# Entering the first layer by quarters of its features, and summing the adaLN modulation on column strips of TensorE

## The chip, the cores and the metric

One Trainium2 chip, one core of it. The metric is the time of one execution of the whole kernel on the device, in microseconds (us), as the median of several runs. The profiled execution is one run more, taken by the hardware profiler.

TensorE is written PE here (PEld is its loading of weights), VectorE is DVE, ScalarE is ACT, GpSimd is POOL, and SP is the queue that issues most of the DMAs.

## The reference

The kernel computes two stacked blocks on 256 tokens of 1024 features, all in float32. The first block has two layers, and the change touches only the modulation and the norm at their entry, above all that of layer 0:

```python
def first_block(x, c, ada_w, ada_b, norm_g, ab_w_in, ...):
    cs = jax.nn.silu(c)                                  # c: 1 x 1024
    for layer in range(2):
        mod = cs @ ada_w[layer] + ada_b[layer]           # ada_w[layer]: 1024 x 3072
        shift, scale, gate = jnp.split(mod, 3, axis=-1)
        h = rms_norm(x, norm_g[layer]) * (1.0 + scale[:, None, :]) + shift[:, None, :]
        if layer % 2 == 0:
            y = even_mixer(h, ab_w_in[0], ab_w_out[0], ...)   # qa,ka,va | qb,kb,vb | g, two attentions
        else:
            y = odd_mixer(h, c_w_in[0], c_w_out[0], c_sink[0])
        x = x + gate[:, None, :] * y
    return rms_norm(x, final_g)
```

The second block (four mixers, then a gated FFN, twice) is not touched.

## The kernel before

**Matrix products.** Activations lie transposed, features on the 128 partitions in 8 chunks (`act`: a pair hi, lo of [128, 8, 256]). Each product of two float32 matrices is three matmuls on pairs of a rounded part and its remainder (`mm3`, L238 to L240). A weight unit of 128x1024 is fetched by SP into `wr`, rounded by ACT into `wh` (L220), and its remainder `wl` is a subtraction on DVE (L221). Products with features as output rows have 256 columns, those with tokens as output rows have 512.

**Order.** A scheduler writes down one order of instructions for each engine and for SP ahead of time, by priority; an engine then runs its list strictly in order, and an instruction whose input is late holds up all that stands behind it. Buffers rotate in pools: a new tile waits until the last reader of the buffer's earlier content is done. Small PSUM tiles (`mx`) come from a pool of 4 banks, products (`mm`) from one of 4.

**Modulation of layer 0, shift and scale** (`Mod.start`). It runs in two halves of 512 features. Rows of `ada_w` come in tiles of 128 rows x 512 columns (half 0: two row chunks in one DMA of 512 KB). Each row chunk k is to be multiplied by cs of its 128 rows and summed over k and over the partitions. The shift's chunks are summed over k on DVE (first chunk L434, then L436, an instruction of 128x512 each); of the scale's 8 chunks in half 0, the first 6 are summed on PE (L472; `csB` holds cs broadcast to 128 columns, so every output row is the full sum), the others on DVE. A matmul with ones (L481) then sums over the partitions and spreads the row to all partitions. norm_g of layer 0 is spread by a ones matmul too (L419, `gb`). G = norm_g*(1+scale) and the shift so stand as [128, 1024] tiles.

**First norm and first products** (`even_layer`). In each half, xn = x * rstd * G + shift (L597, L599) is built in pieces of 2 chunks by 2 token tiles, transposed on PE (L317), and split into hi (ACT, L321) and lo (DVE, L322). Then follow the products qa, ka (`proj_fm_part`) and va (`proj_tok_part`) over the 4 chunks of this half; the second half goes on adding to the same PSUM banks. After that the first attention begins with `sc` (L364, softmax on DVE L370 and ACT L373), `pt` (transposes of p, L382) and `pv` (L645), between products of qb, kb, vb and the gate.

**Later parts** (`Mod.part`): the gate of layer 0, and scale, shift and gate of layer 1, each in two halves. They are called one after the other from `later` while the attentions run: layer 0's gate and layer 1's scale and shift, 6 halves, in the even layer, layer 1's gate in the odd one. Each half fetches 8 tiles of 128x512 (`aw`, 3 buffers), sums them on DVE (L434, L436) into `macc`, adds the row of ada_b on POOL (L491), and ends with a ones matmul (L495).

**Layer 1's norm** (`AdaNorm`) uses layer 1's G and shift in row form, transposes at L317, and starts the odd layer's products.

Of the kernel before, what the change touches and what calls it, by code (L numbers as in the profile page):

```python
# [32 lines left out]
for _n, _l in ROWS:  # L33
# [4 lines left out]
        ("rwkv_r_k_2", 4), ("rwkv_v0_2", 2), ("hgrn_lb_logits_2", 4)]  # L38
# [318 lines left out]


# [45 lines left out]
class Mod:  # L404


    def __init__(self, n, l):
        self.n, self.l = n, l
        self.G = n.s2(f"G{l}", tag="mod")
        if l == 0:  # L410

            for half in range(2):
                s = slice(half * 512, half * 512 + 512)
                g = n.par("g1")[0:1, :]
                r = n.a["rows"]
                n.nc.scalar.dma_start(g, bass.AP(tensor=r.tensor, offset=r.offset + ROW_OFF["norm_g"] + half * 512,
                                                 ap=[[1, 1], [1, 512]]))
                ps = n.mx("gb")
                n.nc.tensor.matmul(ps, lhsT=n.ones[0:1, :], rhs=g, start=True, stop=True)  # L419
                n.nc.scalar.copy(self.G[:, s], ps)  # L420
        else:
            n.row_bc(self.G, "norm_g", l * D, D)
        self.shift, self.gate = n.s2(f"shift{l}", tag="mod"), n.s2(f"gate{l}", tag="mod")

    def src(self, part, half, k, m):
        w = self.n.a["ada_w"]
        ap = [[3 * D, 128], [128 * 3 * D, m], [1, 512]] if m > 1 else [[3 * D, 128], [1, 512]]
        return bass.AP(tensor=w.tensor, ap=ap,
                       offset=w.offset + self.l * D * 3 * D + k * 128 * 3 * D + part * D + half * 512)

    def add_k(self, acc, k, w, first):
        n, nc = self.n, self.n.nc
        if first:
            nc.vector.tensor_scalar(acc, w, n.cs[:, k:k + 1], None, op0=OP.mult)  # L434
        else:
            nc.vector.scalar_tensor_tensor(acc, w, n.cs[:, k:k + 1], acc, op0=OP.mult, op1=OP.add)  # L436
# [18 lines left out]
    def start(self, half, then=None):  # L455

        n, nc = self.n, self.n.nc
        bb = [self.row(part, half) for part in range(2)]
        ps = [n.mx("mod"), n.mx("mod")]
        acc = [n.s2("macc", tag="bias") for _ in range(2)]  # L460
        m, pe = (1, 0) if half else (2, 6)
        for k in range(0, 8, m):
            for part in (0, 1):
                if half:
                    rv = n.s2("aw").unsqueeze(1)
                else:
                    p, tag = (n.p_hi, "hi") if part else (n.p_lo, "lo")
                    rv = v2(p.tile([128, 1024], F32, name="aw", tag=tag))
                nc.sync.dma_start(rv if m > 1 else rv[:, 0, :], self.src(part, half, k, m))
                for j in range(k, k + m):  # L470
                    if part and j < pe:
                        nc.tensor.matmul(ps[1], lhsT=n.csB[:, j * 128:j * 128 + 128], rhs=rv[:, j - k, :],  # L472
                                         start=(j == 0), stop=False)
                    else:
                        self.add_k(acc[part], j, rv[:, j - k, :], j == pe * part)
                        if j == pe * part:
                            nc.vector.tensor_add(acc[part][0:1, :], acc[part][0:1, :], bb[part])
            if k == 2 and then:
                then()
        for part in (1, 0):  # L480
            nc.tensor.matmul(ps[part], lhsT=n.ones, rhs=acc[part], start=not (part and pe), stop=True)  # L481
            self.finish(part, half, ps[part])

    def part(self, part, half):
        n, nc = self.n, self.n.nc
        acc = n.s2("macc", tag="macc")
        for k in range(8):
            w = n.s2("aw", tag="aw")
            nc.sync.dma_start(w, self.src(part, half, k, 1))
            self.add_k(acc, k, w, k == 0)  # L490
        nc.gpsimd.tensor_add(acc[0:1, :], acc[0:1, :], self.row(part, half))  # L491

        def finish():
            ps = n.mx("mod")
            nc.tensor.matmul(ps, lhsT=n.ones, rhs=acc, start=True, stop=True)  # L495
            self.finish(part, half, ps)
        return finish

# [61 lines left out]
def even_layer(n, mod, later, follow):  # L560
# [24 lines left out]

    qk = [[n.mm() for _ in range(2)] for _ in range(2)]
    xn = [n.big("xn") for _ in range(2)]
    rs = []
    va = []
    for half in range(2):  # L590
        mod.start(half, None if half else n.load_x)
        if half == 0:
            rs = [n.norm_stat(t, xn[t]) for t in range(2)]
        for k in range(half * 4, half * 4 + 4, 2):
            s = slice(k * 128, k * 128 + 256)
            for t in range(2):
                nc.vector.scalar_tensor_tensor(xn[t][:, s], n.x[:, t, s], rs[t], mod.G[:, s], op0=OP.mult,  # L597
                                               op1=OP.mult)
# [1105 lines left out]
```

## Time and profile before

| what | value |
|---|---|
| median of 3 runs | 1337.56 us (1334.25 to 1338.48) |
| the profiled execution | 1340.15 us, of which the span from the first to the last instruction is 1338.4 us |
| PE busy | 1275.9 us, 95% of the span |
| DVE busy | 843.1 us, 63% |
| ACT busy | 647.6 us, 48% |
| POOL busy | 66.2 us, 5% |
| chain that ended last | PE 69%, DVE 9%, issue 5%, DMA 3% |
| TensorE's granted clock, mean | 0.987 |

A granted clock of 1 is 2.4 GHz and the lower level, 1.2 GHz, is 0.5; a mean between them says what share of the time was spent at each. The chain of work that ended last is followed back from the last instruction, at each step to what released it. In rows of the trace, `mm<-hh,wh` is an instruction that writes tile mm from hh and wh, `128*128` the rows and columns of the array that it uses, and `x4` says that four are shown as one row.

### The profile page before, as it was taken

The page shows a single profiled execution, that of the slowest core. Times are in us where ns is not written, and L with a number is a line of the kernel's source. Part 1 is how long each engine was busy: PE and PEld are TensorE (multiplying, and loading weights), DVE is VectorE, ACT ScalarE, POOL GpSimd, SP SyncE. Part 2 cuts the span into 40 slices and gives each one's busy share as a digit, 9 for nine tenths or more (in the row PEclk, how much of TensorE's full clock was granted, in tenths as well). Part 3 has the DMA queues.
Part 4 walks back from the last instruction along what each step waited for, and adds up shares of the span by engine and source line. Part 5 has one row for each costly group of instructions (what it writes and reads, how often), then busy time and mean ns, then how long its engine had stood idle before and what let it go on. Part 6 is the DMA issues. An engine that isn't in the chain of part 4 may idle for free.

```text
span 1338.4 us, 20297 instructions
## 1 busy us (share of the span) xinstructions
PE 1275.9 (95%) x7824; PEld 1101.6 (82%) x7824; DVE 843.1 (63%) x1438; ACT 647.6 (48%) x1093; POOL 66.2 (5%) x82
## 2 busy tenths in 40 slices
PE   6888889999899999999999999999999999999997
PEld 3777667888788888888899987988888887899986
DVE  6876897666658754666655544657753756655543
ACT  3364645665655345444544443556244444644432
POOL 0011110000111000000000000010000000000000
PEclk8898999999999999999999999999999999999999
DMA  8887765644552332365565554742331464655552
GB/s 303 302 268 269 245 215 181 200 141 131 173 167 87 105 96 90 103 215 180 174 186 183 181 188 142 229 146 91 94 112 64 149 199 155 201 179 186 186 186 86
DMA packets 104956, 227.19 MB, mean 170 GB/s; under 512 B 8206, under 2 KB 8350, under 8 KB 104860
## 3 DMA queue, kind: packets, MB, share of 16 engines
q1 hardware_dynamic: 102560, 219.18, 50.9%
q0 software_dynamic: 1984, 6.60, 1.9%
q8 instruction: 61, 1.00, 0.3%
q14 instruction: 35, 0.29, 0.1%
q10 hardware_dynamic: 316, 0.12, 0.0%
HBM read 224.82 MB, written 1.05 MB: 169 GB/s over the span
## 4 chain that ended last, share of the span: by engine, by line
PE 69%; DVE 9%; issue 5%; DMA 3%; ACT 2%; POOL 1%; DVEq 0%; POOLq 0%; ACTq 0%; SPq 0%
PE mm L240 19%; PE mm L239 19%; PE mm L238 19%; DVE wl L221 2%; PE p L1386 2%; PE p L1392 2%; DMA aw<-in_ada_w_dram 1%; PE sc L364 1%; PE pv L815 1%; ACT wh L220 1%; DMA wr<-in_gu_dram 1%; PE hs L1115 1%; PE cm L364 1%; DVE macc L436 1%; DMA wr<-in_ab_w_out_dram 1%
## 5 line engine op out<-in xcount | busy, mean ns | idle before, releaser
L221 DVE TENSOR_TENSOR wl<-wr,wh 128x1024 fp32r<-128x1024 f32 (+1 forms) x372 | 433.4, 1171 | 284.8 <-ACT wh L220 282.3
L220 ACT CAST wh<-wr 128x1024 fp32r<-128x1024 f32 (+1 forms) x372 | 369.7, 1002 | 422.2 <-PE mm L240 191.9
L238 PE MATMUL mm<-hh,wh 128*128 128x256 f32 x1104 | 314.9, 287 | 0.9 <-ACT hh L321 0.9
L239 PE MATMUL mm<-hl,wh 128*128 128x256 f32 x1104 | 315.3, 286 | 0.0
L240 PE MATMUL mm<-hh,wl 128*128 128x256 f32 x1104 | 314.9, 286 | 0.0
L238 PEld LDWEIGHTS mm<-hh,wh 128*128 128x128 f32 x1104 | 213.6, 194 | 2.7 <-ACT hh L321 1.7
L239 PEld LDWEIGHTS mm<-hl,wh 128*128 128x128 f32 x1104 | 213.7, 194 | 1.2 <-issue 1.0
L240 PEld LDWEIGHTS mm<-hh,wl 128*128 128x128 f32 x1104 | 213.7, 194 | 0.4 <-issue 0.3
L238 PE MATMUL mm<-wh,hh 128*128 128x512 f32 (+1 forms) x480 | 190.2, 397 | 1.0 <-ACT hh L321 0.6
L239 PE MATMUL mm<-wl,hh 128*128 128x512 f32 (+1 forms) x480 | 190.4, 397 | 0.4 <-DVE wl L221 0.4
L240 PE MATMUL mm<-wh,hl 128*128 128x512 f32 (+1 forms) x480 | 189.0, 394 | 0.5 <-DVE hl L322 0.5
L238 PEld LDWEIGHTS mm<-wh,hh 128*128 128x128 f32 x480 | 90.7, 189 | 19.4 <-ACT hh L321 1.7
L240 PEld LDWEIGHTS mm<-wh,hl 128*128 128x128 f32 x480 | 90.7, 189 | 18.6 <-DVE hl L322 1.4
L239 PEld LDWEIGHTS mm<-wl,hh 128*128 128x128 f32 x480 | 90.8, 189 | 18.1 <-DVE wl L221 1.2
L238 PE MATMUL mm<-wh,ff 128*128 128x512 f32 x176 | 69.5, 395 | 0.0
L239 PE MATMUL mm<-wl,ff 128*128 128x512 f32 x176 | 69.5, 395 | 0.0
L240 PE MATMUL mm<-wh,ff 128*128 128x512 f32 x176 | 69.4, 395 | 0.0
L436 DVE SCALAR_TENSOR_TENSOR macc<-aw,cs,macc 128x512 f32<-128x512 f32 x78 | 57.3, 748 | 16.1 <-DMA aw<-in_ada_w_dram 15.6
L373 ACT ACTIVATE p<-p,nm 128x256 f32<-128x256 f32 (+1 forms) x80 | 39.6, 496 | 23.7 <-DVE nm L370 23.4
L239 PE MATMUL mm<-wl,yTh 128*128 128x512 f32 x128 | 50.7, 397 | 0.0
L238 PE MATMUL mm<-wh,yTh 128*128 128x512 f32 x128 | 50.5, 403 | 0.0
L240 PE MATMUL mm<-wh,yTl 128*128 128x512 f32 x128 | 50.4, 395 | 0.0
(394 smaller groups left out, 1655.9 us busy)
## 6 DMA issues: line engine op xcount, KB each, us to landing
wr<-in_w_in_dram SPq DMA_DIRECT2D x120, 512.0 KB, 4.2
wr<-in_gu_dram SPq DMA_DIRECT2D x88, 512.0 KB, 4.3
wr<-in_w_ffn_down_dram SPq DMA_DIRECT2D x44, 512.0 KB, 4.2
aw<-in_ada_w_dram SPq DMA_DIRECT2D x80, 256.0 KB, 4.6
wr<-in_ab_w_in_dram SPq DMA_DIRECT2D x32, 512.0 KB, 6.1
wr<-in_c_w_in_dram SPq DMA_DIRECT2D x20, 512.0 KB, 4.6
wr<-in_w_branch_dram SPq DMA_DIRECT2D x16, 512.0 KB, 4.3
wr<-in_w_out_dram SPq DMA_DIRECT2D x16, 512.0 KB, 4.1
```

The costliest lines, as they stand in the source:

```text
L220: nc.scalar.copy(hi[:, i:i + m], raw[:, i:i + m])
L221: nc.vector.tensor_sub(lo[:, i:i + m], raw[:, i:i + m], hi[:, i:i + m].bitcast(F32))
L238: mm(out, lhsT=ah, rhs=bh, start=start, stop=False, **kw)
L239: mm(out, lhsT=ah, rhs=bl, start=False, stop=False, **kw)
L240: mm(out, lhsT=al, rhs=bh, start=False, stop=stop, **kw)
L364: self.nc.tensor.matmul(out, lhsT=lhsT, rhs=rhs, start=True, stop=True)
L373: nc.scalar.activation(p, p, AF.Exp, bias=nm, scale=-1.0, accum_out=l)
L436: nc.vector.scalar_tensor_tensor(acc, w, n.cs[:, k:k + 1], acc, op0=OP.mult, op1=OP.add)
L815: nc.tensor.matmul(o, lhsT=pT[:, kc * 256 + t * 128:kc * 256 + t * 128 + 128], rhs=tok[kc][:, g * 64:g * 64 + 64], start=(kc == 0), stop=( ...
L1115: mm(o.rearrange("p (a n b) -> p a n b", a=2, b=b), lhsT=key[:, p, s], rhs=qz, start=True, stop=True)
L1386: mm(half(p1[c], h), lhsT=aT(c, h), rhs=zsel(X[c][:, hd(h)], z, 0), start=True, stop=True)
L1392: mm(half(p3, h), lhsT=t1[c][:, hd(h)], rhs=zsel(Y[c][:, hd(h)], z, 1), start=True, stop=True)
```

## The change

The first layer is entered in four quarters of two feature chunks each. x is fetched first (`load_x` ahead of everything), is multiplied by its rstd and transposed at once (16 transposes, L507 of the changed file) into `xT`, which waits for no modulation. For each quarter q, `FirstNorm.fetch` brings 8 tiles of 128 rows x (256 columns of shift, 256 of scale) in rows of 1 KB; `quarter` sums them on PE: `ada_sum` (L361) is a float32 matmul with a stationary tile `csT[:, k, :]` of 128x32, whose first column is cs of chunk k and whose others are zero, on the column strip 32*(k % 4) of the array, so that four chunks k go to four strips, and chunks k and k+4 add up in the same 32 rows of PSUM. The result is copied to `acc` (ACT one half, DVE the other), four small matmuls (L522) sum it over the partitions into four columns `adac`, and two short DVE instructions add ada_b and multiply norm_g. Since features lie on the partitions, shift and G are now columns: hi is one ACT instruction with scale and bias, and a DVE multiply-add and a DVE subtraction give lo. Then come the products of this quarter.

In `Mod.part`, the sums of layer 0's gate and of layer 1's scale and shift go to PE by `ada_sum` as well; ACT copies the PSUM bank to `macc`, and the row of ada_b is added on DVE, no longer on POOL. Layer 1's gate stays on DVE. `aw` has 5 buffers for 3, `macc` 1 for 2, `mod` 3 for 4.

```diff
+    def ada_sum(self, ps, k, w):
+        g = (k % 4) * 32
+        self.nc.tensor.matmul(ps[g:g + 32, :], lhsT=self.csT[:, k, :], rhs=w, start=(k < 4), stop=(k >= 4))
...
-    def start(self, half, then=None):
...
-        m, pe = (1, 0) if half else (2, 6)
-        for k in range(0, 8, m):
-            for part in (0, 1):
...
-                    if part and j < pe:
-                        nc.tensor.matmul(ps[1], lhsT=n.csB[:, j * 128:j * 128 + 128], rhs=rv[:, j - k, :],
-                                         start=(j == 0), stop=False)
-                    else:
-                        self.add_k(acc[part], j, rv[:, j - k, :], j == pe * part)
...
     def part(self, part, half):
         n, nc = self.n, self.n.nc
         acc = n.s2("macc", tag="macc")
+        row = self.row(part, half)
+        pe = not (self.l and part == 2)
+        ps = n.mx("ada") if pe else None
         for k in range(8):
             w = n.s2("aw", tag="aw")
-            nc.sync.dma_start(w, self.src(part, half, k, 1))
-            self.add_k(acc, k, w, k == 0)
-        nc.gpsimd.tensor_add(acc[0:1, :], acc[0:1, :], self.row(part, half))
+            nc.sync.dma_start(w, self.src(part, half, k))
+            if pe:
+                n.ada_sum(ps, k, w)
...
+        if pe:
+            nc.scalar.copy(acc, ps)
+        nc.vector.tensor_add(acc[0:1, :], acc[0:1, :], row)
...
+class FirstNorm:
...
+    def fetch(self, q, tile):
+        n = self.n
+        w = n.a["ada_w"]
+        for k in range(8):
+            t = tile(k)
+            n.nc.sync.dma_start(v2(t), bass.AP(tensor=w.tensor, offset=w.offset + k * 128 * 3 * D + q * 256,
+                                               ap=[[3 * D, 128], [D, 2], [1, 256]]))
+            self.w[q, k] = t
+
+    def transposed(self):
+        n, nc = self.n, self.n.nc
+        for t in range(2):
+            xn = n.big("xn")
+            r = n.norm_stat(t, xn)
+            for j in range(2):
+                s = slice(j * 512, j * 512 + 512)
...
+                for i in range(4):
+                    c = slice(i * 128, i * 128 + 128)
+                    nc.tensor.transpose(ps[:, c], xn[:, j * 512 + i * 128:j * 512 + i * 128 + 128], n.ident)
...
+    def quarter(self, q):
+        n, nc = self.n, self.n.nc
+        hi, lo = self.act
+        ps = n.mx("ada")
+        for k in range(8):
+            n.ada_sum(ps, k, self.w[q, k])
+        acc = n.s2("macc", tag="macc")
+        nc.scalar.copy(acc[:, 0:256], ps[:, 0:256])
+        nc.vector.tensor_copy(acc[:, 256:512], ps[:, 256:512])
+        pc = n.mx("adac")
+        for i in range(4):
+            nc.tensor.matmul(pc[:, i:i + 1], lhsT=acc[:, i * 128:i * 128 + 128], rhs=n.ones[:, 0:1], start=True,
+                             stop=True)
+        m = n.col(6, "mod")
+        nc.vector.tensor_tensor(v2(m[:, 0:4]), v2(pc[:, 0:4]), v2(self.b)[:, :, q * 2:q * 2 + 2], op=OP.add)
+        nc.vector.tensor_tensor(m[:, 4:6], m[:, 2:4], n.ccol("norm_g", q * 2, 2), op=OP.mult)
+        for j in range(2):
+            k = q * 2 + j
+            t = n.g2("ht")[:, 0:256]
+            nc.vector.tensor_scalar(t, self.xT[:, k, :], m[:, 4 + j:5 + j], m[:, j:j + 1], op0=OP.mult, op1=OP.add)
+            nc.scalar.activation(hi[:, k, :], self.xT[:, k, :], AF.Identity, scale=m[:, 4 + j:5 + j],
+                                 bias=m[:, j:j + 1])
+            nc.vector.tensor_sub(lo[:, k, :], t, hi[:, k, :].bitcast(F32))
...
+    n.load_x()
+    first = FirstNorm(n, act)
...
+    first.fetch(0, beside)
+    first.transposed()
     qk = [[n.mm() for _ in range(2)] for _ in range(2)]
...
+    for q in range(4):
+        if q:
+            first.fetch(q, lambda k: n.s2("aw"))
+        first.quarter(q)
         for i, (nm, sc) in enumerate((("qa", -0.125), ("ka", None))):
-            n.proj_fm_part(act, w, i * 512, fm_done(nm, sc), half * 4, half * 4 + 4, qk[i])
...
+            n.proj_fm_part(act, w, i * 512, fm_done(nm, sc), q * 2, q * 2 + 2, qk[i])
+        n.proj_tok_part(act, w, 1024, tok_done("va"), q * 2, q * 2 + 2, va)
...
-    n.csB = n.ng("csB")
-    nc.vector.tensor_copy(n.csB.rearrange("p (a b) -> p a b", a=8), bc(cs.unsqueeze(2), [128, 8, 128]))
+    n.csT = n.p_const.tile([128, 8, 32], F32, name="csT")
+    nc.gpsimd.memset(n.csT, 0.0)
+    nc.vector.tensor_copy(n.csT[:, :, 0:1], cs.unsqueeze(2))
...
-    with n.phase(mod=(4, D), aw=(3, 512), macc=(2, 512), bias=(3, 512), p=(4, 512), pT=(2, 512), yp=(8, 256),
+    with n.phase(mod=(3, D), aw=(5, 512), macc=(1, 512), bias=(3, 512), p=(4, 512), pT=(2, 512), yp=(8, 256),
```

What the scheduler makes of it on the engines, at three places. The first is PE from the program's start. Before, it reads (`gb` is norm_g spread, `mod` the modulation's sums, `tr` the transposes of xn):

```order
L419 MATMUL gb<-g_130,cst 128x512
L419 MATMUL gb<-g_135,cst 128x512
L472 MATMUL mod<-aw,csB 128x512 x6
L481 MATMUL mod<-macc,cst 128x512 x2
L317 MATMUL tr<-cst,xn 128x128 x4
L238 MATMUL mm<-hh,wh 128x256 x4
```

and in the changed kernel, with the end of quarter 0's products and the start of quarter 1:

```order
L507 MATMUL tr<-cst,xn 128x128 x16
L361 MATMUL ada<-aw,csT 32x512 x8
L522 MATMUL adac<-cst,macc 128x1 x4
L238 MATMUL mm<-hh,wh 128x256 x4
...
L240 MATMUL va<-wh,hl 128x512
L361 MATMUL ada<-aw,csT 32x512 x8
L522 MATMUL adac<-cst,macc 128x1 x4
L361 MATMUL ada<-aw,csT 32x512 x4
L238 MATMUL mm<-hh,wh 128x256 x4
```

The transposes moved ahead of the sums; a quarter's sums stand behind the whole of the quarter before, and some sums of the next quarter stand between the small matmuls and the products. In quarters 2 and 3, 4 and 3 of the 8 sums are left to stand there, and between them 4 and 5 went ahead.

The second place is PE in the first attention, where `pv`, `pt` and `sc` alternate with products. Before:

```order
L645 MATMUL pv<-va,pT 128x64 x2
L382 MATMUL pt<-cst,p 128x128
L364 MATMUL sc<-ka,qa 128x256 x4
L645 MATMUL pv<-va,pT 128x64 x2
L382 MATMUL pt<-cst,p 128x128 x3
L238 MATMUL mm<-hh,wh 128x256
```

In the changed kernel, where `ada` is a later part's sum and `mod` the ones matmul that ends a part:

```order
L681 MATMUL pv<-va,pT 128x64 x2
L465 MATMUL mod<-macc,cst 128x512
L681 MATMUL pv<-va,pT 128x64 x2
L361 MATMUL ada<-aw,csT 32x512
L369 MATMUL sc<-ka,qa 128x256 x4
L681 MATMUL pv<-va,pT 128x64 x2
L361 MATMUL ada<-aw,csT 32x512 x4
L387 MATMUL pt<-cst,p 128x128 x4
L238 MATMUL mm<-hh,wh 128x256
```

The 48 sums of the six parts are strewn into PE's list in 29 places: 23 stand alone between other work, and the others stand in groups of 5, 5, 5, 4, 4 and 2.

The third is DVE in the first attention (`p,nm` is the softmax's first step, `rl` its reciprocal, `wl` a weight's remainder). Before:

```order
L221 TENSOR_TENSOR wl<-wr,wh 128x1024
L630 RECIPROCAL rl<-l 128x1
L370 ISA p,nm<-sc,bias 128x256
L370 ISA nm 128x1
L436 SCALAR_TENSOR_TENSOR macc<-aw,cs,macc 128x512
L630 RECIPROCAL rl<-l 128x1
```

In the changed kernel, at about the same softmax steps:

```order
L375 ISA p,nm<-sc,bias 128x256
L375 ISA nm 128x1
L461 TENSOR_TENSOR macc<-macc,adab 1x512
L666 RECIPROCAL rl<-l 128x1
L221 TENSOR_TENSOR wl<-wr,wh 128x1024
```

The sums are gone from DVE's list there, and one row of ada_b for each half part has come in.

## Rows read from the trace of the kernel before

**Rows 1.** Busy time by stage: length, engines' busy us (instructions), granted clock, DMA share, GB/s.
```profile
0.00:82.00 82.00, 63.24 (x297) 47.24 (x297) 61.72 (x119) 31.11 (x54) 6.99 (x14) 0.90 0.86 300
82.00:228.00 146.00, 129.81 (x715) 105.50 (x714) 116.54 (x251) 78.07 (x178) 21.56 (x24) 0.95 0.73 233
```

**Rows 2.** PE's waits, 0 to 82 us: in total, times, longest.
```profile
PE gb L419 <- DMA g<-in_rows_dram: 6.3, 1, 6.3
PE tr L317 <- issue: 3.1, 1, 3.1
```

**Rows 3.** PE's timeline, 8 to 27 us: start, us, what, idle before.
```profile
26.07 1.23 PE L238 MATMUL mm<-hh,wh 128*128 128x256 f32 x4 [0.46 <-ACT hh L321]
```

**Rows 4.** Gigabytes a second that the DMAs moved, 0 to 60 us in 40 slices.
```profile
GB/s 0 119 332 362 383 354 386 366 407 408 406 410 408 404 366 29 225 307 255 296 265 182 315 300 386 309 268 298 303 276 332 399 190 330 173 359 320 164 321 205
```

**Rows 5.** PEld's timeline, 9 to 17.6 us: the 128x512 float32 products of L472.
```profile
12.70 0.34 PEld L472 LDWEIGHTS mod<-aw,csB 128*128 128x128 f32 x1 [0.52 <-issue]
13.55 0.34 PEld L472 LDWEIGHTS mod<-aw,csB 128*128 128x128 f32 x1 [0.52 <-issue]
...
16.05 0.19 PEld L472 LDWEIGHTS mod<-aw,csB 128*128 128x128 f32 x1 [0.24 <-issue]
16.48 0.19 PEld L472 LDWEIGHTS mod<-aw,csB 128*128 128x128 f32 x1 [0.24 <-issue]
```

**Rows 6.** ACT's instructions by line, 0 to 82 us: count, busy us, mean ns.
```profile
L321 ACT CAST hh<-tr 128x256 fp32r<-128x256 f32 x8 | 3.0, 372 | 6.9 <-PE tr L317 6.8
```

**Rows 7.** PE's timeline, 84.9 to 89 us: products of 256 columns.
```profile
87.77 0.28 PE L240 MATMUL mm<-hh,wl 128*128 128x256 f32 x1
87.89 0.28 PE L238 MATMUL mm<-hh,wh 128*128 128x256 f32 x1
```

**Rows 8.** PE's timeline, 81 to 82.6 us: products of 512 columns, first transposes of p.
```profile
81.39 0.40 PE L239 MATMUL va<-wl,hh 128*128 128x512 f32 x1
81.62 0.39 PE L240 MATMUL va<-wh,hl 128*128 128x512 f32 x1
...
82.00 0.66 PE L382 MATMUL pt<-cst,p 128*128 128x128 f32 x4
```

**Rows 9.** Stages with a low granted clock, columns as in rows 1.
```profile
20.00:30.00 10.00, 6.14 (x24) 4.85 (x25) 8.18 (x16) 5.33 (x9) 0.00 (x0) 0.72 0.73 262
...
99.00:112.00 13.00, 8.78 (x55) 8.41 (x54) 5.47 (x15) 4.93 (x13) 0.57 (x1) 0.74 0.80 267
```

**Rows 10.** PE's timeline: row halves of the array (sc), one column strip (pvl).
```profile
68.21 1.14 PE L364 MATMUL sc<-ka,qa 64*128 64x256 f32 x8 [0.48 <-ACT ka L570]
...
889.73 1.05 PE L1229 MATMUL pvl<-shift,v 128*32 128x256 f32 x4
```

**Rows 11.** PE's timeline, 889 to 892.3 us: another tile shape between products.
```profile
891.17 0.28 PE L239 MATMUL mm<-hl,wh 128*128 128x256 f32 x1
891.38 0.69 PE L1236 MATMUL pvm<-vl,v 32*128 32x256 f32 x2
892.01 0.39 PE L240 MATMUL mm<-hh,wl 128*128 128x256 f32 x1
```

**Rows 12.** DVE's instructions by line, 82 to 228 us: count, busy us, mean ns, idle before.
```profile
L436 DVE SCALAR_TENSOR_TENSOR macc<-aw,cs,macc 128x512 f32<-128x512 f32 x47 | 35.2, 748 | 12.4 <-DMA aw<-in_ada_w_dram 12.2
```

**Rows 13.** DVE's timeline, 97 to 103.5 us.
```profile
102.68 0.75 DVE L436 SCALAR_TENSOR_TENSOR macc<-aw,cs,macc 128x512 f32<-128x512 f32 x1 [5.42 <-DMA aw<-in_ada_w_dram]
```

**Rows 14.** PE's waits, 82 to 228 us.
```profile
PE pv L645 <- ACT ya L649: 4.2, 1, 4.2
PE tr L317 <- DVE xn L512: 2.5, 1, 2.5
PE tr L554 <- DVE yb L551: 2.0, 1, 2.0
PE tr L554 <- DVE ya L551: 2.0, 1, 2.0
PE pt L382 <- DVE p L693: 1.8, 1, 1.8
```

More of the change, by code (lines that the diff above doesn't have):

```diff
@@ L408, in __init__, with src @@
         self.n, self.l = n, l
[L409 to L420, printed above, removed]
-        else:
+        if l:
+            self.G = n.s2(f"G{l}", tag="mod")
             n.row_bc(self.G, "norm_g", l * D, D)
-        self.shift, self.gate = n.s2(f"shift{l}", tag="mod"), n.s2(f"gate{l}", tag="mod")
-    def src(self, part, half, k, m):
+            self.shift = n.s2(f"shift{l}", tag="mod")
+        self.gate = n.s2(f"gate{l}", tag="mod")
+    def src(self, part, half, k):
         w = self.n.a["ada_w"]
-        ap = [[3 * D, 128], [128 * 3 * D, m], [1, 512]] if m > 1 else [[3 * D, 128], [1, 512]]
-        return bass.AP(tensor=w.tensor, ap=ap,
+        return bass.AP(tensor=w.tensor, ap=[[3 * D, 128], [1, 512]],
                        offset=w.offset + self.l * D * 3 * D + k * 128 * 3 * D + part * D + half * 512)
[L431 to L436, printed above, removed]
     def finish(self, part, half, ps):
@@ L453, in row @@
         return bb[0:1, :]
-    def start(self, half, then=None):
[L457 to L460, printed above, removed]
-        m, pe = (1, 0) if half else (2, 6)
-        for k in range(0, 8, m):
-            for part in (0, 1):
[L464 to L470, printed above, removed]
-                    if part and j < pe:
-                        nc.tensor.matmul(ps[1], lhsT=n.csB[:, j * 128:j * 128 + 128], rhs=rv[:, j - k, :],
-                                         start=(j == 0), stop=False)
-                    else:
-                        self.add_k(acc[part], j, rv[:, j - k, :], j == pe * part)
[L476 to L482, printed above, removed]
     def part(self, part, half):
@@ L497, in part, with __init__ @@
         return finish
+class FirstNorm:
+    def __init__(self, n, act):
+        nc = n.nc
+        self.n, self.act = n, act
+        self.xT = n.p_act.tile([128, 8, S], F32, name="xT", tag="acth")
+        self.b = n.p_const.tile([128, 16], F32, name="adab1")
+        nc.vector.tensor_copy(self.b[:, 0:8], n.ccol("ada_b", 0, 8))
+        nc.vector.tensor_scalar(self.b[:, 8:16], n.ccol("ada_b", 8, 8), 1.0, None, op0=OP.add)
+        self.w = {}
+    def fetch(self, q, tile):
[13 more added lines that the diff above has]
+                s = slice(j * 512, j * 512 + 512)
+                if j:
+                    nc.scalar.activation(xn[:, s], n.x[:, t, s], AF.Copy, scale=r)
+                else:
+                    nc.vector.tensor_scalar(xn[:, s], n.x[:, t, s], r, None, op0=OP.mult)
+                ps = n.mx("tr")
+                for i in range(4):
+                    c = slice(i * 128, i * 128 + 128)
+                    nc.tensor.transpose(ps[:, c], xn[:, j * 512 + i * 128:j * 512 + i * 128 + 128], n.ident)
+                o = self.xT[:, j * 4:j * 4 + 4, t * 128:t * 128 + 128]
+                (nc.vector.tensor_copy if j else nc.scalar.copy)(o, v4(ps))
+    def quarter(self, q):
[21 more added lines that the diff above has]
+            nc.vector.tensor_sub(lo[:, k, :], t, hi[:, k, :].bitcast(F32))
@@ L583, in tok_done, with beside @@
         return done
-    qk = [[n.mm() for _ in range(2)] for _ in range(2)]
[L587 to L598, printed above, removed]
-                nc.vector.tensor_add(xn[t][:, s], xn[t][:, s], mod.shift[:, s])
-                n.to_T(xn[t][:, s], t, act, k, 2)
-        for i, (nm, sc) in enumerate((("qa", -0.125), ("ka", None))):
-            n.proj_fm_part(act, w, i * 512, fm_done(nm, sc), half * 4, half * 4 + 4, qk[i])
-        if half == 0:
-            va = [n.mx("va"), n.mx("va")]
-        n.proj_tok_part(act, w, 1024, tok_done("va"), half * 4, half * 4 + 4, va)
-    n.load_masks(xn[1][:, 512:])
+    n.load_x()
+    first = FirstNorm(n, act)
+    pool = {}
+    def beside(k):
+        if k % 2 == 0:
+            p, tag = (n.p_hi, "hi") if k % 4 else (n.p_lo, "lo")
+            pool[0] = p.tile([128, 1024], F32, name="aw", tag=tag)
+        return pool[0][:, (k % 2) * 512:(k % 2) * 512 + 512]
+    first.fetch(0, beside)
+    first.transposed()
+    qk = [[n.mm() for _ in range(2)] for _ in range(2)]
+    va = [n.mx("va"), n.mx("va")]
+    for q in range(4):
+        if q:
+            first.fetch(q, lambda k: n.s2("aw"))
+        first.quarter(q)
+        for i, (nm, sc) in enumerate((("qa", -0.125), ("ka", None))):
+            n.proj_fm_part(act, w, i * 512, fm_done(nm, sc), q * 2, q * 2 + 2, qk[i])
+        n.proj_tok_part(act, w, 1024, tok_done("va"), q * 2, q * 2 + 2, va)
+    n.load_masks(act[1][:, 7, :].bitcast(F32))
     sg = {}
```

6 lines of the change are left out of this document (5 added, 1 removed).

## The prediction

> **What bounds the kernel now.** I read the table by stage first, because PE is busy for 95% of the whole span and that mean hides where it is not. Two stages are touched: the entry, from 0 to 82 us, and the even layer's attentions up to the first products of the odd layer, 82 to 228 us. In the entry PE is busy for 63.2 of 82 us and the DMAs move 300 GB/s; in the attentions PE is busy for 129.8 of 146 us, at a mean granted clock of 0.95 [rows 1]. So the entry is a chain of waits, and the attention stage is nearly a PE stage. Then I read PE's waits in each stage. In the entry, PE's first 6.3 us go to norm_g's row and 3.1 us pass before the first transposes [rows 2]; the first product starts only at 26.07 us [rows 3], and the last of the entry's work ends at 82.00, where the first transposes of p begin [rows 8]. In the attentions the longest wait, 4.2 us, is for ACT's `ya` [rows 14]. Its cause is one engine further back: DVE stands for 5.42 us at a sum that waits for an `aw` DMA [rows 13], with the softmax's steps queued behind it, and PE's list comes to `pv`. Around it the granted clock falls to a mean of 0.74 over 13 us [rows 9]; as the levels are 1.2 and 2.4 GHz, about 0.26 x 13 = 3.4 us more are lost there.
>
> **The entry, step by step.** Before, nothing can be multiplied until scale and shift are there in row form. After, I count as follows. In the table of DMA slices (1.5 us each) 1 MB has come by about 5.5 us and 3 MB by about 11 us [rows 4]; x is the first of it and quarter 0's 2 MB of `ada_w` the rest, with about 1 us to land: 12.3. The 16 transposes fit in between (statistics and scaling take until about 9, then 16 at the cold 0.21, my estimate from a 128x128 tile's share of the cold step below). A 128x512 float32 product consists of two records, 0.43 us apart warm and 0.85 apart cold [rows 5], so 0.86 or 1.71 us. Eight sums on four strips, if four strips run together, are two rounds: cold 3.4, ending at 16. Then a copy of 256 columns (0.4, as the cast of that size, 0.372 [rows 6]), four small float32 matmuls with their loads (1.8 cold, estimate), two short DVE steps and the hi instruction (1.1 with hand-overs, the hand-over before the first product being 0.46 [rows 3]). The first product starts at about 19.3, against 26.07.
>
> A quarter's products are 48 of 256 columns, 0.12 us apart [rows 7], and 12 of 512 columns, 0.23 apart [rows 8]: 5.8 + 2.7 = 8.5 us. Quarter 0 gets 2.5 more for the low clock that the same place shows now (0.72 over 10 us, 2.8 lost [rows 9]): it ends at 30.5. Between two quarters PE's list has the next sums behind the last product, so their chain lies bare: 8 sums 1.7, a change of tile shape 0.27 (below), copy 0.65 with hand-over, small matmuls 1.1, columns and hi 1.1: 4.8 us; for quarters 2 and 3, part of whose sums went ahead, 4.7 and 4.1, because the sums put in behind the small matmuls take time too. So 30.5 + 13.6 + 3 x 8.5 + 0.9 (scores in between) = 70.5, say **71 against 82: 11 us gained**. The 1 KB rows of the fetches (twice as many packets as now) cost DMA time, which nothing waits for at this pace: some 16 MB by 66 us is under the present 300 GB/s.
>
> **The later parts.** DVE loses 47 of its sums in this stage, at 748 ns 35.2 us [rows 12], and gains a 1-row add of some 0.67 us per half part. PE gains 48 sums. Two costs are not in the trace. First, whether column strips run together: no row shows two. The nearest rows: products on two row halves run together (eight records of `sc` in 1.14 us, about 0.14 each), while four records on one and the same column strip take 1.05, no less than 0.2 each [rows 10]. I take full overlap of neighbours on different strips, by the row halves; none is the other bound. Second, the price of a lone sum between other shapes. In the row where two small records stand between products, 891.17 to 892.01 is 0.84 us [rows 11], of which the product before takes 0.12 and the two records of 256 columns 2 x 0.216 (the step of the strip's records in the view of [rows 10]); 0.29 is left, and I take 0.27 for a visit. A lone sum then costs 0.86 + 0.27 = 1.13 us. Of the 29 places, 23 hold one sum: 26.0. The groups of five cost two rounds, 2.0 each; those of four and of two one round, 1.13: 9.4 in all. **Added on PE: 35.4 us** (41.3 + 7.8 = 49.1 without any overlap; 27.6 if a visit is free).
>
> What goes: PE's waits in this stage are 146 - 129.8 = 16.2 us, and the clock's 0.05 x 146 = 7.3 more, 23.5 together. Those that DVE's sums make or lengthen go, I think: the `ya` wait and its clock (4.2 + 3.4), the other wait for `ya` (2.0) and that for p (1.8): 11.4 us. Those that stay have another cause: layer 1's norm behind the output projection (2.5) and yb (2.0) [rows 14] are chains that no sum stands in, with the low clock behind each. **Sum: -11 + 35.4 - 11.4 = +13 us.** After 228 us the order is as before, and layer 1's gate still runs on DVE: 0. Against the profiled execution's 1340.15 that is 1353.2; the median of the runs lies 2.6 lower, so 1350.5.
>
> A new wait is possible too: a sum stands in PE's list and waits for its `aw` tile, as DVE's did for 5.42 us, now with products queued behind it. With 5 buffers for 3 I put 0 to 4 us, and 0 in the sum.
>
> **A rule weighed.** The row of one strip shows its records 0.2 us apart with a weight load between them that costs nothing visible [rows 10]. The Trainium skill, "TensorE: Matmul & The Clock Gate", Part 3, The mechanism, says that a weight load overlaps a running matmul only where the row group differs; sums on column strips all use the same rows. By that rule each of the 96 records would add its load of about 0.1 us: some 10 us more. The trace speaks against it where one strip is used twice, and has no row for two strips. The same section's table has three column strips 2.38 times as fast as one, an estimate by which groups would cost 2 to 3 us more than in my sum.
>
> **The rivals.**
> (A) The forecast: strips overlap, 11 us come at the entry, PE's list grows by 35, some waits go. 1350.5; with the entry's gain between 8 and 14, the visits between 0.15 and 0.35 and the waits that go between 7 and 16: 1339 to 1361.
> (B) Strips do not overlap, or by half. For it: no row shows it. Then each quarter's sums take 6.9 us and not 1.7; about 5 in each of the four lie bare, the entry ends at 91, and the later sums cost 49: 9 + 49 - 13 = +45, 1382. Half of it: 1365.
> (C) The other side: PE's waits were nearly all DVE's doing, and with 35 us off DVE and sums to fill PE's list they all go. -11 + 35.4 - 23.5 = +0.9 with my visits; with free visits (27.6) it is -7, 1331. It ends faster than before if waits and visits together give back more than 28 us where I have 11.4. For it: DVE is busy for 116.5 of the 146 us [rows 1], hardly less than PE. Against it: the waits behind layer 1's norm and yb hang on PE's own products, and sums can't stand in a wait that they aren't placed in.
> (D) Nothing to measure: the two sides cancel to within 0.3%, about 4 us, which is what a measurement here can tell from no change: 1333.5 to 1341.5.
> (E) Loads that are not hidden, by the rule above: 48 sums of two records with 0.1 us each, +10 on (A): 1360.
>
> **How the numbers follow.** (A) outside of (D)'s window 0.47, (B) 0.12 with its half, (E) 0.05, (C) 0.20, (D) 0.16. The likeliest is (A), 1350.5. Slower is A + B + E = 0.64, faster C = 0.20, same D = 0.16. The range reaches from (C) with half its free visits, 1330, to (B)'s half and a little beyond, 1372: below it some of (C), above it the full (B). The likeliest case's own range is 1339 to 1361.
>
> **What would show it.** Right: the first product near 19 us; the first transposes of p near 71; L361's records in groups of four starting together, eight in 1.7 to 2 us warm; lone sums 1.1 us between their neighbours; DVE without L436 in the even layer; PE's 4.2 us wait gone; layer 1's transposes some 12 us later than now, and all after them shifted by as much. Wrong: L361's records each 0.43 us behind the last (B); PE's busy share in the attentions near 1 and layer 1's norm earlier than now (C); PE waiting for `aw` (the new wait); first products later than 26 us, if the column form's chain is longer than I count.

## The result, and the profile of the changed kernel

The change makes the kernel slower, by 1.4%: a median of 1355.51 us (1353.85 to 1357.29, 4 runs) against 1336.36 us (1334.25 to 1338.48, 4 runs), a ratio of 1.0143, with a 95% interval of 1.0120 to 1.0166. That is +19.2 us where +13 was forecast; 1355.5 lies in the range and in the likeliest case's own range. The two profiled executions, from which the tables below are made, differ by 16.0 us (1340.15 and 1356.13). That the sum came so near is partly luck: over the same work, the entry gave back 5 us and not 11, the attentions cost 21 and not 24, and the two errors have opposite signs.

The table by stage is cut at two marks, the first transposes of p (82.00 us before, 79.15 now) and the first transposes of layer 1's norm. Before the change, beside the entry's row in [rows 1]:

```profile
82.00:213.79 131.79, 116.14 (x653) 94.80 (x652) 104.65 (x232) 72.33 (x168) 20.08 (x22) 0.96 0.75 238
213.79:1338.40 1124.61, 1096.49 (x6876) 959.53 (x6876) 676.74 (x1089) 544.21 (x871) 39.14 (x46) 1.00 0.48 152
```

and after it, columns as in [rows 1]:

```profile
0.00:79.15 79.15, 61.62 (x379) 48.61 (x380) 36.01 (x82) 35.24 (x58) 6.50 (x15) 0.92 0.88 300
79.15:229.74 150.59, 145.81 (x740) 95.42 (x739) 76.70 (x196) 74.96 (x176) 9.01 (x13) 1.00 0.66 209
229.74:1354.40 1124.66, 1095.96 (x6876) 959.51 (x6876) 683.08 (x1100) 544.44 (x872) 39.73 (x47) 1.00 0.50 153
```

By these marks the entry is 2.9 us shorter, the attentions are 18.8 longer, and the rest is equal to 0.1 us. But PE's list has not the same content ahead of the first mark: behind the last product of va, one product of the next weights stands ahead of it before, and ten in the changed kernel. The start of va's last product, 81.62 before and 76.47 now, has the same products, scores and transposes ahead of it in both. The changed kernel's list at this place, where [rows 8] has the one of before:

```profile
76.47 0.74 PE L240 MATMUL va<-wh,hl 128*128 128x512 f32 x1
77.01 0.41 PE L238 MATMUL mm<-hh,wh 128*128 128x256 f32 x1
...
79.15 1.01 PE L387 MATMUL pt<-cst,p 128*128 128x128 f32 x4
```

Cut at va's last product, the attentions read, before and after:

```profile
81.62:213.79 132.17, 116.52 (x654) 94.99 (x653) 104.97 (x232) 72.65 (x169) 20.08 (x22) 0.96 0.75 239
```

```profile
76.47:229.74 153.27, 148.49 (x751) 98.00 (x750) 77.94 (x203) 77.45 (x180) 9.01 (x13) 0.99 0.66 211
```

So the entry is 5.1 us shorter and the attentions are 21.1 longer. In the attentions PE went from 116.5 busy of 132.2 us to 148.5 of 153.3 us, and its clock from 0.96 to 0.99: it hardly waits any more, and it has too much to do. DVE's 27 us less bought the end of PE's waits, and no more.

PE's timeline at the entry of the changed kernel:

```profile
11.59 2.76 PE L361 MATMUL ada<-aw,csT 128*32 128x512 f32 x16
15.97 0.61 PE L522 MATMUL adac<-cst,macc 128*128 128x1 f32 x4 [1.62 <-ACT macc L518]
17.30 0.61 PE L522 MATMUL adac<-cst,macc 128*128 128x1 f32 x4 [0.72 <-DVE macc L519]
21.31 1.22 PE L238 MATMUL mm<-hh,wh 128*128 128x256 f32 x4 [3.41 <-ACT hh L531]
...
31.77 1.92 PE L361 MATMUL ada<-aw,csT 128*32 128x512 f32 x16
...
36.47 0.74 PE L238 MATMUL mm<-hh,wh 128*128 128x256 f32 x4
```

Column strips do run together: eight sums, 16 records, take 1.92 us at 31.77, where 16 records 0.43 us apart would take 6.9. The sums end at 14.35, but the first product ([rows 3] before) starts at 21.31, after waits of 1.62, 0.72 and 3.41 us. What stood in the way is in the lists of ACT and DVE:

```profile
14.60 1.04 ACT L220 CAST wh<-wr 128x1024 fp32r<-128x1024 f32 x1 [3.17 <-DMA wr<-in_ab_w_in_dram]
15.55 0.37 ACT L518 COPY macc<-ada 128x256 f32<-128x256 f32 x1
...
19.59 1.04 ACT L220 CAST wh<-wr 128x1024 fp32r<-128x1024 f32 x1 [1.19 <-DMA wr<-in_ab_w_in_dram]
20.66 1.09 ACT L531 ACTIVATE hh<-xT,mod 128x256 fp32r<-128x256 f32 x2
```

```profile
15.68 1.23 DVE L221 TENSOR_TENSOR wl<-wr,wh 128x1024 fp32r<-128x1024 f32 x1 [3.29 <-ACT wh L220]
16.82 0.42 DVE L519 COPY macc<-ada 128x256 f32<-128x256 f32 x1
18.44 1.32 DVE L221 TENSOR_TENSOR wl<-wr,wh 128x1024 fp32r<-128x1024 f32 x1 [1.20 <-ACT wh L220]
19.68 0.15 DVE L525 TENSOR_TENSOR mod<-adac,adab 128x4 f32<-128x4 f32 x1
```

Each short step of quarter 0 stands behind a weight's cast or subtraction, and these wait for their own DMA. The small matmuls of 17.30 are done at 17.9, and the columns that need them are made at 19.68.

PE's three longest waits from 70 to 260 us of the changed kernel, against [rows 14] (of the first, 1.4 us lie ahead of layer 1's first transposes, the rest behind them):

```profile
PE tr L317 <- DVE xn L548: 2.9, 2, 1.5
PE ada L361 <- DMA aw<-in_ada_w_dram: 1.4, 3, 1.1
PE pt L387 <- DVE p L729: 1.4, 1, 1.4
```

The waits for `ya` and for `yb` are gone or small; that for `aw`, the new one, is 1.4 us. PE's timeline around a lone sum, and one around a group of four:

```profile
99.26 1.06 PE L361 MATMUL ada<-aw,csT 128*32 128x512 f32 x8
100.26 0.66 PE L387 MATMUL pt<-cst,p 128*128 128x128 f32 x4
...
103.62 0.36 PE L238 MATMUL mm<-hh,wh 128*128 128x256 f32 x1
103.91 1.05 PE L361 MATMUL ada<-aw,csT 128*32 128x512 f32 x2
104.89 0.39 PE L239 MATMUL mm<-hl,wh 128*128 128x256 f32 x1
```

Four sums (8 records) and one sum (2 records) hold PE equally long, 1.0 us from their start to the next instruction's. Of the lone sum, three strips of the array stand unused. From 103.62 to 104.89 is 1.27 us, of which the product takes 0.12: 1.15 for the lone sum, where I had 1.13. All 96 records of the later parts together, by PE's instructions by line in this stage:

```profile
L361 PE MATMUL ada<-aw,csT 128*32 128x512 f32 x96 | 33.1, 604 | 1.4 <-DMA aw<-in_ada_w_dram 1.4
```

33.1 us by this row alone, where I had 35.4 with what a visit costs its neighbours.

### The profile page after: what moved, and what is told of

It is laid out like the page before. It is cut to its first block, busy times and chain, and to the rows that moved or that the text cites. A ratio compares the mean times of both kernels' runs of the same rounds, so it can differ in the third digit from the quotient of the medians.

```text
span 1354.4 us, 20528 instructions
## 1 busy us (share of the span) xinstructions
PE 1303.4 (96%) x7992; PEld 1103.5 (81%) x7992; DVE 795.8 (59%) x1376; ACT 654.6 (48%) x1103; POOL 55.2 (4%) x75
## 3 DMA queue, kind: packets, MB, share of 16 engines
HBM read 224.84 MB, written 1.05 MB: 167 GB/s over the span
## 4 chain that ended last, share of the span: by engine, by line
PE 78%; DVE 8%; issue 5%; DMA 4%; ACT 3%; POOL 1%; SPq 0%; POOLq 0%; ACTq 0%; DVEq 0%
PE mm L238 20%; PE mm L240 20%; PE mm L239 20%; PE ada L361 3%; DVE wl L221 2%; PE p L1423 2%; ACT wh L220 2%; PE p L1429 1%; DMA wr<-in_ab_w_in_dram 1%; PE sc L369 1%; PE pv L851 1%; PE pt L387 1%; PE hs L1152 1%; PE cm L369 1%; PE tr L317 1%
## 5 line engine op out<-in xcount | busy, mean ns | idle before, releaser
L361 PE MATMUL ada<-aw,csT 128*32 128x512 f32 x160 | 42.9, 604 | 1.4 <-DMA aw<-in_ada_w_dram 1.4
```

The lines of the kernel that those rows point to most:

```text
L361: self.nc.tensor.matmul(ps[g:g + 32, :], lhsT=self.csT[:, k, :], rhs=w, start=(k < 4), stop=(k >= 4))
```

## The experiments

My theory: the loss is the 48 sums in the list of a PE that was nearly full, most of them alone on one strip of four. The rivals: that the entry's new form is the loss; that the strips do not help; that PE is held by what the sums bring along (their DMAs, copies and rows).

**One half of the change at a time.** `e1_entry_only` puts the later parts back on DVE, with the `aw` and `macc` buffers of before:

```diff
-            if pe:
-                n.ada_sum(ps, k, w)
+            self.add_k(acc, k, w, k == 0)
...
-        nc.vector.tensor_add(acc[0:1, :], acc[0:1, :], row)
+        nc.gpsimd.tensor_add(acc[0:1, :], acc[0:1, :], self.row(part, half))
...
-aw=(5, 512), macc=(1, 512)
+aw=(3, 512), macc=(2, 512)
```

> The quarters at the entry are kept; the later parts' sums go back to DVE, their rows to POOL, with 3 aw and 2 macc buffers. The sums on PE are the loss: the first transposes of p come at about 79 us as in the changed kernel (82 before), PE's waits of the kernel before return in the attentions, and the time is 1333.5 us (1329 to 1338), some 22 less than changed. Rival, that the entry's form, its small DMA rows or its pools are the loss: 1345 or more.

Measured: 1337.17 us, ratio to before 1.0009 (0.9995 to 1.0023). The rival falls, the loss is gone with the sums. But the entry's gain is gone too. The first transposes of p come at 77.14, 4.9 us earlier than before, and layer 1's first transposes at 213.09, only 0.7 earlier. PE's waits in between, and below them DVE's from 120 to 168 us:

```profile
PE pt L387 <- DVE p L725: 5.6, 2, 3.9
PE pv L677 <- ACT ya L681: 3.5, 2, 2.1
```

```profile
DVE macc L448 <- DMA aw<-in_ada_w_dram: 4.1, 4, 2.4
```

PE waits for DVE's softmax, and DVE for the sums' tiles, as in [rows 13]. The waits are not all of it: the stage is 4.2 us longer than before by the same marks (with one product ahead of the first in both), and 1.7 of that is PE's idle time, 17.3 us for 15.7. The other 2.5 are longer busy time of as many records.

`e2_parts_only` keeps the entry of before and has only the later sums on the strips:

```diff
     def part(self, part, half):
...
+            if pe:
+                n.ada_sum(ps, k, w)
...
+        if pe:
+            nc.scalar.copy(acc, ps)
+        nc.vector.tensor_add(acc[0:1, :], acc[0:1, :], row)
...
-aw=(3, 512), macc=(2, 512)
+aw=(4, 512), macc=(1, 512)
```

> The entry of the kernel before; only the later parts' sums go to PE's column strips (4 aw buffers, since csB and csT stand together). The sums on PE are the loss: the attentions take some 18.7 us longer than before, 1355 us (1349 to 1360). Rival, the entry is the loss: 1340 or less.

Measured: 1362.40 us, ratio 1.0181 (1.0165 to 1.0196): 25 us slower than before, a little above my range. Without the new entry the sums make the whole loss, and some more. In the stage, 80.03 to 231.45 us, PE is full:

```profile
80.03:231.45 151.42, 148.09 (x747) 95.95 (x745) 74.34 (x188) 74.75 (x171) 8.59 (x13) 1.00 0.65 203
```

The changed kernel is 6.9 us faster, but that is not the worth of its entry alone. In the profiles, which differ by 6.1 us, it starts va's last product 3.3 us earlier (76.47 against 79.79) and layer 1's first transposes 1.7 us earlier. The other 4.4 come behind them, where e2 takes 1129.0 us and the changed kernel 1124.7; e2 has one `aw` buffer less, and whether that makes them was not tried.

**Do the strips help?** `e3_one_strip` puts all sums on one strip, and only the 32 rows that this fills are copied and summed over the partitions:

```diff
-        g = (k % 4) * 32
-        self.nc.tensor.matmul(ps[g:g + 32, :], lhsT=self.csT[:, k, :], rhs=w, start=(k < 4), stop=(k >= 4))
+        self.nc.tensor.matmul(ps[0:32, :], lhsT=self.csT[:, k, :], rhs=w, start=(k == 0), stop=(k == 7))
```

> All sums on one and the same column strip, accumulated over eight chunks into 32 rows; the rest as in the changed kernel. If neighbours on four strips run together, that is lost: the groups' 25 sums cost 23 us for 9.4, and eight sums at the entry 6.9 for 1.9, most of it bare: 1355.5 + 14 + 15 = 1385 us (1375 to 1393). Rival, that strips give nothing: 1355 as changed, since lone sums cost the same on any strip.

Measured: 1388.77 us, ratio 1.0382 (1.0366 to 1.0398), as expected. The eight sums at the entry and the later 96 records on one strip (two views, PE's timeline and its instructions by line):

```profile
11.97 7.93 PE L360 MATMUL ada<-aw,csT 128*32 128x512 f32 x16
```

```profile
L360 PE MATMUL ada<-aw,csT 128*32 128x512 f32 x96 | 44.4, 597 | 0.9 <-DMA aw<-in_ada_w_dram 0.9
```

Strips take 5.2 us off quarter 0's sums (7.93 against 2.76), but only 11.3 of 44.4 off the later ones, since most of those have no neighbour.

**Does it pay to bring neighbours together?** `e4_fours1` fetches four chunks at once into one buffer:

```diff
-            w = n.s2("aw", tag="aw")
-            nc.sync.dma_start(w, self.src(part, half, k))
+            if k % 4 == 0:
+                w4 = n.s2("aw", tag="aw").rearrange("p (a b) -> p a b", a=4)
+                nc.sync.dma_start(w4, self.src(part, half, k))
+            w = w4[:, k % 4, :]
...
-aw=(5, 512)
+aw=(1, 2048)
```

> The later parts fetch four chunks in one DMA of 1 MB into one buffer of 128x2048, so their sums come in 17 visits to PE's list (12 of four sums, five of them split 1 and 3) and not in 29. If the price is the lone sum's time and visit, 17 x 1.13 = 19 us in place of 35: 1339 us (1334 to 1346). Rival, that PE is held by something else that the sums bring (their DMAs' place in the queue, the copies on ACT, the rows on DVE): 1350 or more. Layer 1's gate shares the one buffer and may stall DVE by a few us.

Measured: 1350.18 us, ratio 1.0086 (1.0062 to 1.0110). This is 5 us faster than the changed kernel, and by the time alone it is the rival's number. By stage it is not: from the first transposes of p to layer 1's takes 139.1 us (77.39 to 216.51) in place of 150.6, and what follows takes 1133.9 where every other kernel so far had 1122 to 1129. Of these 9 us more than in the changed kernel, one wait of PE in the odd layer makes 4.7:

```profile
PE pv L854 <- ACT pT L389: 4.7, 1, 4.7
```

`e5_fours_apart` gives layer 1's gate tiles of its own, and the sums a higher priority:

```diff
+                with n.lazily(-3000):
+                    n.ada_sum(ps, k, w4[:, k % 4, :])
+                continue
+            w = n.s2("awg", tag="awg")
+            nc.sync.dma_start(w, self.src(part, half, k, 1))
...
-aw=(1, 2048)
+aw=(1, 2048), awg=(2, 512)
```

> As e4_fours1, but layer 1's gate has two 128x512 buffers of its own, and the sums of a 1 MB tile have a higher priority: 16 visits to PE's list in the even layer. If e4_fours1 lost its gain in the odd layer, by DVE waiting for the one buffer, the end moves up by the 9 us that stand there: 1341 us (1336 to 1345). Rival, that fewer visits don't pay as counted: 1348 or more.

Measured: 1347.07 us, ratio 1.0068 (1.0044 to 1.0092): 8 us faster than the changed kernel, not the 14 expected, and just short of the rival's 1348. The stage itself went as counted:

```profile
L361 PE MATMUL ada<-aw,csT 128*32 128x512 f32 x96 | 16.9, 604 | 2.5 <-DMA aw<-in_ada_w_dram 2.5
```

```profile
78.27:215.54 137.27, 130.29 (x743) 95.19 (x742) 76.97 (x200) 74.65 (x176) 7.82 (x13) 0.99 0.69 226
```

The same 96 records cost 16.9 us in 16 visits and 33.1 in 29; the stage is 13.3 us shorter. The price of the visits is thereby shown: as many sums, with fewer of them alone, take less of PE. What follows layer 1's first transposes still takes 1129.6 us, 5 more than in the changed kernel, and PE waits 2.4 us at the same `pv`. That two buffers are too few for layer 1's gate is my reading; it wasn't tried with more.

**The price of a lone sum.** `e7_full_width` has the later sums on the whole array, without a change of tile shape:

```diff
-                n.ada_sum(ps, k, w)
+                nc.tensor.matmul(ps, lhsT=n.csW[:, k * 128:k * 128 + 128], rhs=w, start=(k == 0), stop=(k == 7))
```

> The later parts' sums use a stationary tile of 128x128 (cs in column 0, zeros elsewhere) on the whole array in place of the strips; entry as changed. 48 sums take 48 x 0.86 = 41.3 us. If a lone sum on a strip costs 0.27 for the change of tile shape, the strips' list costs 35.4 and the time grows by 6: 1361 us (1358 to 1365). If the change of shape costs nothing, the strips' list costs 27.6 and the time grows by 14: 1369.

Measured: 1365.37 us, ratio 1.0201 (1.0161 to 1.0240), +9.9 to the changed kernel: between the two, and above my interval for the first by a little. In its profile the stage is 5.1 us longer (82.85 to 238.56), as forecast with 6, and the entry, which the edit leaves alone, 3.7 later. The sums themselves:

```profile
L454 PE MATMUL ada<-aw,csW 128*128 128x512 f32 x96 | 45.1, 602 | 1.8 <-DMA aw<-in_ada_w_dram 1.8
```

So on strips the 29 visits cost 33.1 - 27.6 = 5.5 us by this column, 0.19 each, without what stands in the neighbours' rows. The full width streams 41.3 - 27.6 = 13.7 us more, so that by the stage's growth of 5.1 a visit costs 0.30, and by the growth of the median, 9.9, it costs 0.13. My 0.27 lies between these, and the run does not settle it more finely.

**The clock at the entry's end.** `e8_fill` runs quarter 3's sums a second time, unread:

```diff
+        if q == 3:
+            sp = n.mx("adaf")
+            for k in range(8):
+                n.ada_sum(sp, k, self.w[q, k])
         m = n.col(6, "mod")
```

> As changed, with quarter 3's eight sums run a second time into a bank that nobody reads, behind its small matmuls, where quarters 1 and 2 have sums of the next quarter. If PE's standing still there is what makes the clock fall in quarter 3's products, they run 0.12 us apart from the first on (0.21 for the first four microseconds as changed) and the first transposes of p come 1 to 2 us earlier though 1.7 us of sums came in. Rival, the clock falls there anyway: the transposes come 0.6 us or more later.

In the changed kernel, PE stands still ahead of quarter 3's first product, and its products are 0.21 us apart from 63.03 until 66.24:

```profile
62.16 0.74 PE L238 MATMUL mm<-hh,wh 128*128 128x256 f32 x4 [1.08 <-ACT hh L531]
...
66.03 0.41 PE L238 MATMUL mm<-hh,wh 128*128 128x256 f32 x1
66.24 0.32 PE L239 MATMUL mm<-hl,wh 128*128 128x256 f32 x1
```

With the fill:

```profile
62.76 1.92 PE L361 MATMUL adaf<-aw,csT 128*32 128x512 f32 x16
64.61 0.39 PE L238 MATMUL mm<-hh,wh 128*128 128x256 f32 x1
64.84 0.28 PE L239 MATMUL mm<-hl,wh 128*128 128x256 f32 x1
64.96 0.28 PE L240 MATMUL mm<-hh,wl 128*128 128x256 f32 x1
```

The granted clock of 58 to 70 us is 1.00 in place of 0.86. From the start of quarter 3's sums to the first transposes of p takes 17.1 us (60.12 to 77.24) in place of 20.8 (58.37 to 79.15). Of these 3.7 us, 1.7 are eight products (0.21 each) that stand ahead of the mark in the changed kernel and behind it here. The clock's part is read from quarter 3's 48 products: they take 5.9 us (64.61 to 70.47) in place of 7.4 (62.16 to 69.51). The run has one time, 1354.57 us, and it cannot be told from the changed kernel's.

**Is there something to keep?** Four more kernels have the quarters and sum the later parts on DVE. `e9_entry_aw5` is e1 with the changed kernel's buffers:

```diff
-aw=(3, 512), macc=(2, 512)
+aw=(5, 512), macc=(1, 512)
```

> As e1_entry_only (quarters at the entry, later sums on DVE), with 5 aw buffers for 3 and 1 macc for 2, as the changed kernel has. If the entry's gain was lost in the attentions to DVE sums that wait for their aw tiles, with the softmax behind them, those waits (4.6 us between 120 and 168 us) shrink, PE's wait of 3.9 us for p goes, and the time is 1333 us (1330 to 1336). Rival, DVE is simply too busy there: 1337 as e1_entry_only.

Measured: 1333.54 us, ratio 0.9978 (0.9963 to 0.9992): faster than the kernel before by 0.2%, and by 22 us than the changed one. DVE's waits for `aw` fell from 10.8 us in e1 to 1.6 over both attentions, PE's for p from 5.6 to 0.9; a new one stands in their place, since with one `macc` the ones matmul waits for POOL's row:

```profile
PE mod L461 <- POOL macc L457: 5.0, 3, 2.4
```

`e10_entry_aw5_fill` adds the fill of e8.

> As e9_entry_aw5, with quarter 3's sums run a second time behind its small matmuls, into a bank that nobody reads, so that PE stands still for less and the clock stays up. If PE's time at the entry's end counts, 1 to 3 us less than e9_entry_aw5: 1331 us. Rival, the attentions swallow it: as e9_entry_aw5.

Measured: 1337.87 us, ratio 1.0024 (1.0005 to 1.0042), 4 us slower than e9. What the fill did for the clock at quarter 3 (1.00 from 60 to 74 us) was lost at once. The scores wait for the softmax, and the first transposes of p start at 82.53 us, where e9 has them at 76.18; further on, PE waits for the same row of POOL's:

```profile
PE mod L461 <- POOL macc L457: 6.4, 2, 5.0
PE sc L369 <- DVE nm L375: 2.9, 1, 2.9
```

`e11_sums_dve` is the changed kernel with the sums alone undone (buffers and the row on DVE as changed), and `e12_sums_dve_aw6` is that with a sixth buffer:

```diff
-            if pe:
-                n.ada_sum(ps, k, w)
+            self.add_k(acc, k, w, k == 0)
...
-        if pe:
-            nc.scalar.copy(acc, ps)
         nc.vector.tensor_add(acc[0:1, :], acc[0:1, :], row)
```

> The changed kernel with one thing undone: the later parts are summed on DVE (entry, 5 aw and 1 macc buffers, the row of ada_b on DVE as changed). If the sums on PE are the whole of the loss, and POOL's add of the row is what PE waits for in e9_entry_aw5 (5.0 us in three waits), this is the fastest: 1330 us (1327 to 1334), 25 less than changed. Rival, the row's 0.67 us on a DVE that is full costs as much as POOL's: 1333.5 as e9_entry_aw5.

> As e11_sums_dve with 6 aw buffers. If DVE's sums still wait for late aw tiles, 1 to 3 us less than e11_sums_dve; if 5 buffers were enough, the same within 2 us.

Measured: e11 1339.10 us, ratio 1.0019 (1.0002 to 1.0035); e12 1333.73 us, ratio 0.9982 (0.9965 to 1.0000). With nothing undone but the engine of the sums, 16.4 of the 19.2 us come back. But my 1330 for e11 was wrong: the row on DVE stands in PE's way as POOL's did (5.3 us in e11 and 3.5 in e12 at the ones matmul, against 5.0 in e9). That e11 is even 5.6 us slower than e9 is not in that wait: from the first transposes of p to layer 1's, its PE is busy for 123.4 us and e9's for 115.9, at a mean clock of 0.92 and 0.97. What made the clock lower there was not tried. The sixth buffer gave back 5.4 us, more than the 1 to 3 that I expected. Moving sums off PE gives up to 22 us back; the entry's quarters leave at most 3 us below the kernel before.

## Why the prediction was right or wrong, point by point

**The entry, 11 us: wrong, 5.1 measured over the same work (2.9 by the first transposes of p).** Two steps were mis-sized. The first product came at 21.31 and not at 19.3: I gave the copy, the columns and hi their own durations and hand-overs, and not the casts and subtractions that stand ahead of them on ACT and DVE and wait for weights. The gaps between quarters came out as counted (4.7 from 31.77 to 36.47, and 3.8 at the last, against 4.8 and 4.1). The rest was left out at the end: from quarter 3's first product at 62.16 to the end of va's last, at 77.01, took 14.9 us, where I had 9.4. The 48 products of quarter 3 took 7.4 us and not 5.8, since the clock fell there; e8 shows it. I counted one group of scores (0.9); behind it stand two more, of four records each, that take 1.05 us each and wait for 0.21 and 0.58. The kernel before has these groups too. The clock falls a second time behind them, from 76.5 to 79.8 us, which costs va's last product 0.3 and the ten products behind it 0.9; this fall is only read from the trace.

**The sums on PE, +35.4: near, 33.1 by the row of L361.** Full overlap on different strips, taken from the row halves of [rows 10], was right (e3). So was the price of a lone sum, 1.13, measured with 1.15 at 103.91, and that the number of visits and not of sums sets it (e5: 16.9 us for the same 96 records).

**The waits that go, 11.4: a little too small.** Over the same work, PE's busy time in the attentions grew by 32.0 us (116.5 to 148.5), which is what I had: 35.4 of sums less 3.4 for the clock. Which part the sums, the clock and the neighbours of the visits have in it, no run separates, so that it fits to a tenth is luck. PE's idle time fell from 15.7 to 4.8 us, by 10.9 with the new wait for `aw` already taken off, where I had 8.0 without the clock. I had left layer 1's norm (2.5) and yb's wait (2.0) among those that stay, and had not counted the wait of the second attention's scores for ACT's `kb` (1.5). Of the first 1.4 us are left, of the second 0.2, and the third is gone; of the wait for p (1.8), which I took to go, 1.4 are left. Rival (C) was right in so far as nearly all of PE's waits went; that it did not decide is because the sums cost more than all of them, and the entry did not bring its 11.

**The new wait for `aw`, 0 to 4: right, 1.4.** **After the stage, 0: right, 0.1.** **Rival (B)**, strips that do not overlap: it exists as e3, at 1388.8, where I had 1382 (its sum takes 13 for the waits where (A) takes 11.4; with that it is 1384). **Rival (E)**, loads that are not hidden: at 31.77, 16 records on four strips, all on the same rows of the array, take 1.92 us; 16 loads of 0.1 added to two rounds of 0.86 would be 3.3. By the rule of the Trainium skill, "TensorE: Matmul & The Clock Gate", Part 3, The mechanism, that loads overlap a running matmul only where the row group differs, they should have shown; the trace doesn't agree for these tiles.

## What to carry to other kernels

Work that is moved off a waiting engine onto the one that bounds the stage is paid in full, while the waits that it removes can be counted beforehand and are the most that it can win: here 33 us of sums stood against 23.5 us of waits and clock. Column strips are free only for neighbours: a lone matmul on one strip holds the whole array as long as four on four strips do (1.0 us each here), so look in the scheduled order for how many stand together, and fetch so that they come together. A gain ahead of a stage need not arrive behind it: of the 4.9 us by which e1 enters the attentions earlier than the kernel before, 0.7 are left at layer 1's first transposes, and of the changed kernel's 3.3 against e2, 1.7. And compare stages only between marks that have the same work ahead of them: here ten products in front of a mark made a gain of 5.1 us look like 2.9.

## What the runs showed of the hardware that I had not expected

The granted clock fell after short pauses of PE. In the changed kernel, PE is idle for 0.59 and 1.08 us around four small matmuls at 60 us; the first products that follow are 0.12 us apart, and from about 62.9 to 66.3 they are 0.21 apart, at 1.2 GHz (a mean of 0.52 from 62.8 to 66.3 us). With 1.9 us of sums that nobody reads in the gap, the clock stayed at 2.4 GHz throughout (1.00 from 58 to 70 us). The other kernels with these pauses, e1, e4, e5, e7, e9, e11 and e12, have the fall too, and e3 and e10, which have 1.9 us of sums in that place, have not (1.00 from 66 to 80 us in e3). In quarters 1 and 2 of the changed kernel, where the next sums stood there, it did not fall either (1.00 from 32 to 58 us).

The entry's end scatters by more than the kernels differ there: kernels with the same entry reached the first transposes of p at 75.8 (e11), 76.2 (e9), 77.1 (e1), 79.2 (changed), 79.5 (e12) and 82.9 us (e7) in their profiles. In the changed kernel and in e7 ten products of the next weights stand ahead of that mark, 2.1 us of these times, and at most one in the others. A comparison of two entries by one profile each is good to a few microseconds only.
